# A two-layer RWKV/conv/Fourier/MoE block: the input projection and its sixteen units put in one fixed order on every queue

## Chip, core and metric

One core of a Trainium2 chip runs the whole block in one launch. The metric is the device time of one execution in microseconds (us). Engines: TensorE (PE; PEld is its weight load), VectorE (DVE), ScalarE (ACT), GpSimd (POOL), and SyncE (SP), which here issues nearly all DMA transfers. All data are float32; the projection runs on pairs of fp32r values.

## The reference, cut to what matters

1024 latent and 256 context tokens, D = 1024, two layers. The change lies in the first half of a layer, up to the recurrent scan:

```python
px = hx @ w_in                      # 1024 -> 2944 columns, 23 blocks of 128
zx = zx + (grid_shift(zx) - zx) * mu_shift
r, k, v, lw_f, lw_b, la_f, la_b, lg = split(zx)
kk = k * k_k; kk = kk / max(norm(kk), 1e-12)          # per head of 64
for dn in 2 directions:
    decay = exp(-exp(-softplus(-(w0 + tanh(lw) @ w2)) - 0.5))
    a     = sigmoid(a0 + la @ a2);  k_dir = k * (1 + (a - 1) * k_a)
    S_t = S_{t-1} diag(decay_t) - (S_{t-1} kk_t)(kk_t * a_t)^T + v_t k_dir_t^T;  y_t = S_t r_t
```

Then gated readout, short convolution, Fourier mixing, output projection, and a mixture of experts, none of which the change touches.

## The kernel before

Each layer goes through stages: input projection with units, scan (the rest of the projection, the convolution and the Fourier part run beside it), output projection, experts, combine. The scan is done in chunks of 64 tokens. What a chunk needs is made ahead in **units**: one unit is one pair of heads (p, four of them), one half of the 1280 tokens (hf) and one direction (d), so 16 units per layer and 10 chunks for each of two heads (e) in a unit.

A unit's steps, all inside `inproj`: `gates` (matmuls of the two low-rank inputs, tanh on ScalarE, scaling and a running sum on VectorE, two exponentials), `heads` (normalised kk, once for two units), `factors` (the operands ar and bk of the chunk products; bk's halves are split between VectorE and GpSimd), `attn` (score matmuls, masked into two tiles X; transposes of bk; the DMA writes of ar, X and bk for the scan). The strictly triangular 64x64 block of each chunk must be inverted: `inverse` takes the two 32x32 diagonal blocks of every chunk of three units from a DRAM scratch image (gD), one block per partition, and inverts them by 30 steps of two operations on GpSimd; it writes the blocks back and a transposed copy to a second image (xD). `merge` reads both for one unit and makes the corner of the 64x64 inverse with two rounds of small matmuls. The last four units' blocks are inverted by VectorE (two) and, beside the scan, GpSimd (two).

Between these the projection runs as a stream (`project`, line 386): 23 blocks of 128 columns, each 24 matmuls for 256 tokens and twice 24 for 512, counted as 0.5 and 1. `Pace` hands them out: `free(n)` issues n of them at once, `feed(n)` ties them behind points that the unit's steps have noted (`point`), and `defer` puts small work a given number of matmuls later. Otherwise the order on each engine is settled by a planner's simulated timeline, SyncE's transfers included. `in_order` (used elsewhere) fixes the order of traced instructions on every engine but SyncE.

Per layer the order is: free until the first heads are there and `Q_FIRST` more, then 16 times a unit with `Q_UNIT` matmuls fed behind it (52 and 35 in layer 0, 49 and 24 in layer 1), then the last `attn`, three merges and `Q_TAIL`. In the pool of tiles, X has two buffers (both used by one unit), ar, bk, E, Ei one each; score products, transposes, heads and gates share two PSUM banks (`bank`).

Of the kernel before, what the change touches and what calls it, by code (L numbers as in the profile page):

```python
# [19 lines left out]
P = 128  # L20
# [20 lines left out]
Q_FIRST, Q_UNIT, Q_TAIL, Q_SCAN, Q_LATE, Q_AT = (40, 35), ((52, 35), (49, 24)), ((40, 60, 40), (20, 60, 40)), 10, 40, (1, 8)  # L41
# [7 lines left out]

Q = 32 * C + 32  # L50
U_ = 2 * Q

# [10 lines left out]
class Pace:  # L63
# [8 lines left out]

    HOLD = 1e9
# [17 lines left out]
    def after(self):  # L91
        return self.tc.issue_after(self.last)

    def one(self, ctx):
        cost = self.cost
        try:
            self.cost = self.stream.send(ctx)
        except StopIteration:
            self.cost = None
        for x in self.later:  # L100
            x[0] -= cost
        while self.later and not self.open and (self.cost is None or self.later[0][0] <= 0):
            self.later.pop(0)[1]()
# [20 lines left out]
class K:  # L124
# [30 lines left out]
    def in_order(self):  # L155
# [128 lines left out]
    def weights(self, l, j):  # L284

        hp = self.hp
        wr = hp.tile([P, KD, P], F32, name="wr")
        self.nc.sync.dma_start(wr, self.a["w_in"][l, j])
# [59 lines left out]
    def inproj(self, l, last):  # L348
# [13 lines left out]
        nc.vector.tensor_scalar(om, self.vec("mu", 0, 15), -1.0, 1.0, op0=OP.mult, op1=OP.add)  # L362
        oka = sp.tile([P, 4], F32, name="oka")
        nc.vector.tensor_scalar(oka, self.vec("ka", 0, 4), -1.0, 1.0, op0=OP.mult, op1=OP.add)
# [21 lines left out]
        def project(j, use, ctx=True):  # L386

            wh, wl = self.pre.pop(j) if j in self.pre else self.weights(l, j)
            for c0, n in NCK if ctx else NCK[1:]:
# [11 lines left out]
                pace.open = False  # L401
                between()

# [32 lines left out]
        def shifted(j, name, bufs=1, ctx=True):  # L436
# [14 lines left out]
            else:  # L451
                nc.gpsimd.memset(z[:, :LC], 0.0)
            ts = slice(0, T) if ctx else slice(LC, T)
            nc.scalar.activation(z[:, ts], z[:, ts], AF.Copy, scale=om[:, j:j + 1])
            nc.vector.scalar_tensor_tensor(z[:, ts], zs[:, ts], self.vec("mu", j), z[:, ts], op0=OP.mult, op1=OP.add)
            return z
# [20 lines left out]
        def heads(p, hf, k, inv):  # L477

            kk = un.tile([P, HT], F32, name="kk", bufs=2)
            nc.gpsimd.tensor_copy(kk.rearrange("q (t e d) -> q t e d", e=2, d=64),  # L480
                                 inv[:, 5 * hf:5 * hf + 5, :, None].to_broadcast([P, 5, 2, 64]))
            ps = bank()
            for t in range(5):
                nc.tensor.matmul(ps[:, t * P:(t + 1) * P], kk[:, t * P:(t + 1) * P], self.ident, start=True, stop=True)
# [7 lines left out]
        def gates(p, hf, d, lw, la):  # L492
# [6 lines left out]
            for i, (w, src, dst) in enumerate(((w2, lw, sg), (a2, la, aa))):  # L499
# [8 lines left out]
                nc.vector.tensor_scalar(dst, dst, 0.5, 0.5, op0=OP.mult, op1=OP.add)  # L508
            rev = slice(None, None, -1) if d else slice(None)
            nc.vector.tensor_tensor_scan(flat(sg)[:, rev], rst, flat(sg)[:, rev], 0.0, op0=OP.mult, op1=OP.add)  # L510
            E = un.tile([P, HC, C], F32, name="E")
            Ei = un.tile([P, HC, C], F32, name="Ei")
            nc.scalar.activation(E, sg, AF.Exp, scale=-CC)
            nc.scalar.activation(Ei, sg, AF.Exp, scale=CC)
            return aa, E, Ei

        def factors(p, hf, d, r, k, kk, g, kds):
            aa, E, Ei = g
            rev = slice(None, None, -1) if d else slice(None)
            e0 = 0 if d else C - 1  # L520
            nc.vector.tensor_copy(self.wc[d][:, p, hf * HC:(hf + 1) * HC], E[:, :, e0])
            kd = un.tile([P, HC, C], F32, name="kd", bufs=2)
            nc.scalar.activation(kd, aa, AF.Identity, bias=oka[:, p:p + 1], scale=self.vec("ka", p))
            nc.vector.tensor_tensor(kd, kd, cv(k, hf), op=OP.mult)
            kds.append(kd)
            nc.vector.tensor_tensor(aa, aa, Ei, op=OP.mult)


            ar = un.tile([P, 2, HC, C], F32, name="ar")
            bk = un.tile([P, HC, 2, C], F32, name="bk")  # L530
            lo, hi = slice(0, 64), slice(64, 128)
# [10 lines left out]
            nc.vector.tensor_tensor(ar[:, 1], cv(r, hf), E, op=OP.mult)  # L542
            if len(kds) == 2:
                nc.gpsimd.tensor_tensor(kds[0], kds[0], kds[1], op=OP.add)
                nc.gpsimd.tensor_tensor(kds[0], kds[0], cv(r, hf), op=OP.mult)
# [3 lines left out]
        def attn(p, hf, d, ar, bk):  # L549

            GR = ((0, 5), (5, 5))
            half = lambda e: slice(64 * e, 64 * e + 64)
            img = slice(hf * HC, (hf + 1) * HC)

            Xs = [un.tile([P, 2, HC, C], F32, name="X", bufs=2) for _ in range(2)]
            for c0, n in ((0, 4), (4, 3), (7, 3)):
                ps = bank().rearrange("q (e c s t) -> q e c s t", e=2, s=2, t=C)
                for c in range(n):
                    for e in range(2):
                        h = half(e)  # L560
                        mm = nc.tensor.matmul(ps[:, e, c], bk[h, c0 + c].rearrange("q s t -> q (s t)"), ar[h, :, c0 + c, :],  # L561
                                              start=True, stop=True)
                pace.point(mm, W_ATTN)
                for e in range(2):
                    mv = msk[:, d, e].rearrange("q (s t) -> q s t", s=2)
                    nc.vector.tensor_tensor(Xs[e][:, :, c0:c0 + n].rearrange("q s c t -> q c s t"), ps[:, e, :n],  # L566
                                            mv[:, None].to_broadcast([P, n, 2, C]), op=OP.mult)
            for e in range(2):
                h, o = half(e), half(1 - e)
                X = Xs[e]  # L570
                sn = "q s (n c) t -> q (s n) (c t)"
                for v, rows in ((ar[h], h), (X[o], o)):
                    nc.sync.dma_start(self.rlD[d][e][img, rows, p, :].rearrange("m q x -> q m x"),
                                      v.rearrange(sn, c=2))
                nc.sync.dma_start(self.abD[d][hf * 5:hf * 5 + 5, h, 1, p, :].rearrange("n q x -> q n x"),
                                  X[h, 1].rearrange("q (n c) t -> q n (c t)", c=2))
                m = (2 * place[p, hf, d] + e) * HC
                nc.sync.dma_start(self.mats(self.gD, m, HC), X[h, 0])

            for c0, n in GR:  # L580
                ps = bank()
# [5 lines left out]
                nc.scalar.activation(bt[:, :n].rearrange("q c t -> q (c t)"), ps[:, :n * P], AF.Copy)  # L587
                ch = slice(hf * HC + c0, hf * HC + c0 + n)
                nc.sync.dma_start(self.btD[d][ch, :, p, :].rearrange("c q x -> q c x"), bt[:, :n])

        def inverse(u0, n, eng, new=None):
# [16 lines left out]
            def finish():  # L608
                if new is None:
                    xt = un.tile([P, 32, 32], F32, name="zt")[:n]  # L610
                    nc.scalar.activation(xt, gt.rearrange("q i a -> q a i"), AF.Copy)
                    nc.sync.dma_start(self.diag(self.gD, j0, n), gt)
                else:
                    xs = [qp.tile([P, 512], F32, name=name)[:n].rearrange("q (a i) -> q a i", i=32)
                          for name in ("pq", "pl")]
                    for x, sl in zip(xs, (slice(0, 16), slice(16, 32))):
                        nc.scalar.activation(x, gt[:, :, sl].rearrange("q i a -> q a i"), AF.Copy)
                    nc.sync.dma_start(self.diag(self.gD, j0, n), gt)
                    xt = gt
                    for x, sl in zip(xs, (slice(0, 16), slice(16, 32))):  # L620
                        nc.scalar.activation(xt[:, sl], x, AF.Copy)
                nc.sync.dma_start(self.diag(self.xD, j0, n), xt)
            return finish

        def merge(u, new, bank="pq"):
# [7 lines left out]
            for e, (r, o) in enumerate(ro):  # L633
                m = (2 * u + e) * HC
                nc.sync.dma_start(AM[64 * e:64 * e + 64], self.mats(self.gD, m, HC))
                nc.sync.dma_start(XP[r], self.mats(self.xD, m, HC)[lo, :, lo])

            def work(ctx):
                for st in range(2):
# [10 lines left out]
                    for e, (r, o) in enumerate(ro):  # L650
                        if st == 0:
                            nc.scalar.activation(XP[o], pq[o], AF.Copy)
                        else:
                            nc.scalar.activation(AM[r, :, hi], pq[r], AF.Copy)
                nc.sync.dma_start(self.abD[d][hf * 5:hf * 5 + 5, :, 0, p, :].rearrange("n q x -> q n x"),
                                  AM.rearrange("q (n c) t -> q n (c t)", c=2))
            return work

        def values(p):

            zo = yield from shifted(8 + p, "v")
            nc.sync.dma_start(self.vT[p], zo)

            def late():
# [12 lines left out]
            pace.defer(Q_LATE, late)  # L677
# [90 lines left out]
        def gate():  # L768
            zo = yield from shifted(14, "v", 1, not last)
            nc.scalar.activation(zo, zo, AF.Sigmoid)  # L770
            nc.sync.dma_start(self.lgT, zo)
        cs_, rks, invs = [], [], []

        def streams(p):
            yield from values(p)
            k = yield from shifted(p + 4, "k", 2)
# [1174 lines left out]
```

## Time and profile before

| | us |
|---|---|
| median of 3 runs (3517.28 to 3523.49) | 3521.67 |
| profiled execution | 3517.43 |
| its span (first to last instruction) | 3515.6 |
| mean granted TensorE clock | 0.926 |
| first gates, last masked X, first scan step, layer 0 | 174.5, 583.1, 638.2 |
| the same, layer 1 | 1968.7, 2364.6, 2427.4 |
| busy: PE, DVE, ACT, POOL (share of the span) | 89%, 65%, 53%, 32% |

A busy share is an average over stages with different limits, so the rows below are cut to the stage of the change. The granted clock is given as a share of full speed. DMA share is the mean busy share of the core's 16 DMA engines. SyncE's instructions are not counted as busy; its waits are listed by themselves. A wait is put down to what came last.

### The profile page before, as it was taken

The page shows a single profiled execution, that of the slowest core. Times are in us where ns is not written, and L with a number is a line of the kernel's source. Part 1 is how long each engine was busy: PE and PEld are TensorE (multiplying, and loading weights), DVE is VectorE, ACT ScalarE, POOL GpSimd, SP SyncE. Part 2 cuts the span into 40 slices and gives each one's busy share as a digit, 9 for nine tenths or more (in the row PEclk, how much of TensorE's full clock was granted, in tenths as well). Part 3 has the DMA queues.
Part 4 walks back from the last instruction along what each step waited for, and adds up shares of the span by engine and source line. Part 5 has one row for each costly group of instructions (what it writes and reads, how often), then busy time and mean ns, then how long its engine had stood idle before and what let it go on. Part 6 is the DMA issues. An engine that isn't in the chain of part 4 may idle for free. (4 is left out here: it accounts for less than half of the span.)

```text
span 3515.6 us, 59528 instructions
## 1 busy us (share of the span) xinstructions
PE 3123.8 (89%) x22452; PEld 2447.4 (70%) x22452; DVE 2274.8 (65%) x3543; ACT 1852.3 (53%) x2856; POOL 1140.5 (32%) x1083
## 2 busy tenths in 40 slices
PE   6998889798898999999979988776988989999996
PEld 3776667577676777788746766565776867778883
DVE  4275566233467899988763465554334879998885
ACT  4343433335333777788753434333353457778883
POOL 0026675411222222333200166664013222233330
PEclk8998888899998999999989999877999989999998
DMA  6668889879755999999956678889896478999996
GB/s 248 213 159 174 185 182 195 229 215 329 228 199 188 363 350 337 369 386 381 369 218 213 177 181 189 176 181 236 231 327 198 154 309 317 348 365 378 377 387 232
DMA packets 708060, 922.36 MB, mean 262 GB/s; under 512 B 335074, under 2 KB 561259, under 8 KB 657852
## 3 DMA queue, kind: packets, MB, share of 16 engines
q1 hardware_dynamic: 669456, 871.05, 77.9%
q0 software_dynamic: 38304, 47.49, 4.0%
q8 instruction: 178, 2.92, 0.3%
q14 instruction: 110, 0.90, 0.1%
q10 hardware_dynamic: 12, 0.00, 0.0%
HBM read 726.92 MB, written 203.23 MB: 265 GB/s over the span
## 5 line engine op out<-in xcount | busy, mean ns | idle before, releaser
L176 DVE TENSOR_TENSOR hl<-ld,hl 128x1024 fp32r<-128x1024 f32 x734 | 892.0, 1267 | 39.4 <-ACT hl L175 37.3
L175 ACT ACTIVATE hl<-ld 128x1024 fp32r<-128x1024 f32 x796 | 793.3, 1058 | 23.9 <-PE pR L1571 15.4
L1571 PE MATMUL pR<-hl,wk 128*128 128x512 f32 x1560 | 455.5, 400 | 0.0
L1571 PE MATMUL pU<-hl,wk 128*128 128x512 f32 x1560 | 446.5, 394 | 0.0
L1595 PE MATMUL pA<-hl,wk 128*128 128x512 f32 x1560 | 388.2, 403 | 12.6 <-DVE wk L176 8.2
L397 PE MATMUL pb<-hh,wh 128*128 128x512 f32 (+1 forms) x1000 | 392.0, 393 | 4.1 <-ACT r L430 1.7
L397 PE MATMUL pb<-hh,wl 128*128 128x512 f32 (+1 forms) x1000 | 385.9, 386 | 6.5 <-DVE wl L176 6.5
L397 PE MATMUL pb<-hl,wh 128*128 128x512 f32 (+1 forms) x1000 | 386.4, 387 | 0.0
L1595 PEld LDWEIGHTS pA<-hl,wk 128*128 128x128 f32 x1560 | 290.6, 191 | 97.1 <-ACT wk L175 19.2
L1571 PEld LDWEIGHTS pU<-hl,wk 128*128 128x128 f32 x1560 | 294.2, 189 | 68.1
L1571 PEld LDWEIGHTS pR<-hl,wk 128*128 128x128 f32 x1560 | 288.1, 189 | 61.4 <-ACT wk L175 0.8
L176 POOL TENSOR_TENSOR hl<-ld,hl 128x1024 fp32r<-128x1024 f32 x62 | 174.1, 2809 | 369.8 <-ACT hl L175 369.8
L1602 POOL DMA_INDIRECT yb<-wk,sca x64 | 101.2, 1581 | 462.3 <-ACT wk L1601 446.7
L397 PEld LDWEIGHTS pb<-hh,wh 128*128 128x128 f32 x1000 | 199.9, 200 | 67.6 <-issue 11.5
L1276 PE MATMUL pA<-hl,wk 128*128 128x512 f32 x864 | 223.1, 408 | 7.3 <-ACT wk L175 7.3
L397 PEld LDWEIGHTS pb<-hh,wl 128*128 128x128 f32 x1000 | 200.1, 200 | 42.3 <-DVE wl L176 6.8
L397 PEld LDWEIGHTS pb<-hl,wh 128*128 128x128 f32 x1000 | 200.3, 200 | 37.5 <-issue 9.6
L1276 PEld LDWEIGHTS pA<-hl,wk 128*128 128x128 f32 x864 | 160.4, 192 | 47.9 <-ACT wk L175 7.8
L1100 POOL DMA_DIRECT2D yD<-yt x72 | 57.9, 805 | 405.3 <-ACT yt L1099 367.8
L1088 DVE TENSOR_TENSOR tm<-pR,ST 128x256 f32<-128x256 f32 x76 | 32.0, 422 | 235.0 <-PE pR L1083 216.6
L175 ACT ACTIVATE wk<-pm 128x256 fp32r<-128x256 f32 (+1 forms) x195 | 89.2, 457 | 177.9 <-PE pm L1585 117.4
L561 PE MATMUL ps<-ar,bk 64*128 64x128 f32 x1280 | 124.5, 334 | 55.9 <-DVE X L566 22.8
(426 smaller groups left out, 5423.3 us busy)
## 6 DMA issues: line engine op xcount, KB each, us to landing
ld<-in_exp_gu SPq DMA_DIRECT2D x260, 1024.0 KB
ld<-in_exp_dn SPq DMA_DIRECT2D x130, 1024.0 KB
st<-rlD SPq DMA_DIRECT2D x80, 512.0 KB
wr<-in_w_in SPq DMA_DIRECT2D x46, 512.0 KB
rlD<-ar SPq DMA_DIRECT2D x64, 320.0 KB
rlD<-X SPq DMA_DIRECT2D x64, 320.0 KB
btD<-bt SPq DMA_DIRECT2D x64, 320.0 KB
st<-abD SPq DMA_DIRECT2D x40, 512.0 KB
```

What stands on the lines that cost most here:

```text
L175: nc.scalar.activation(hi, src, AF.Copy)
L176: (eng or nc.vector).tensor_tensor(lo, src, hi.bitcast(F32), op=OP.subtract)
L397: mm = nc.tensor.matmul(ps[:, :n], w[:, k, :], h[:, k, c0:c0 + n], start=(k == 0 and i == 0), stop=(k == KD - 1 and i == 2))
L561: mm = nc.tensor.matmul(ps[:, e, c], bk[h, c0 + c].rearrange("q s t -> q (s t)"), ar[h, :, c0 + c, :], start=True, stop=True)
L1088: nc.vector.tensor_tensor(tm, RS[:, 1], ST[d], op=OP.add)
L1100: nc.gpsimd.dma_start(self.yD[d][:, ch * C:(ch + 1) * C, :], yt.rearrange("q p d -> q (p d)"))
L1276: nc.tensor.matmul(ps, oo[o][:, k, :], w[k][w_][:, fs], start=(k == 0 and q == 0), stop=(k == KD - 1 and q == 2))
L1571: nc.tensor.matmul(o, x.xT[xi][:, kk, :], w[wi][:, k, :], start=(kk == 0 and i == 0), stop=(kk == KD - 1 and i == 2))
L1595: nc.tensor.matmul(x.y[n], x.h[:, hi_, f, :], dw[wi][:, 0, n * 512:(n + 1) * 512], start=(f == 0 and i == 0), stop=(f == 3 and i == 2))
L1602: nc.gpsimd.indirect_dma_start(out=yb, out_offset=bass.IndirectOffsetOnAxis(ap=x.sca, axis=0), in_=o, in_offset=None, bounds_check=2 * T - ...
```

## The change

Everything from the stream's start to the last merge before the scan is traced inside `in_order(True)`, which now covers SyncE's transfers too. The unit is cut into steps with matmuls of the stream between them (`go`, `free`), and each step belongs to a given unit: the gates of unit u+1, the factors and operands of unit u, the attention of unit u-1, the merge of an earlier unit. GpSimd keeps the inversion alone. The scratch image holds whole 32x32 blocks, one after the other; the transposed image and its writes go, and the merge makes the transpose with one more round of matmuls. X's block is written in six pieces (two diagonal blocks and a corner, for each head). Weights are fetched two blocks ahead and split one block ahead. The shifted input is mixed 24 matmuls after its block. Layer-wide numbers: `Q_FIRST` 40, 35 becomes 20, 0, `Q_LATE` 40 becomes 30.

```diff
-    def in_order(self):
+    def in_order(self, issue=False):
...
-            if i.engine == mybir.EngineType.SP:
+            if i.engine == mybir.EngineType.SP and not issue:
                 continue
...
+                if c0 == (0 if ctx else NCK[1][0]):
+                    if at + 1 in raw:
+                        self.pre[seq[at + 1]] = self.parts(raw.pop(at + 1))
+                    if at and at + 2 < len(seq):
+                        raw[at + 2] = self.fetch(l, seq[at + 2])
...
@@ heads
-            nc.gpsimd.tensor_copy(kk.rearrange("q (t e d) -> q t e d", e=2, d=64),
-                                 inv[:, 5 * hf:5 * hf + 5, :, None].to_broadcast([P, 5, 2, 64]))
...
+                for e in range(2):
+                    nc.tensor.matmul(ps[64 * e:64 * e + 64, t * P:(t + 1) * P],
+                                     inv[:, 5 * hf + t, e:e + 1].to_broadcast([P, 64]), self.ident, start=True, stop=True)
...
@@ gates
-                nc.vector.tensor_scalar(dst, dst, 0.5, 0.5, op0=OP.mult, op1=OP.add)
+                if i == 0:
+                    nc.scalar.activation(dst, dst, AF.Copy, bias=0.5, scale=0.5)
+                yield
...
@@ factors, operands
-            nc.gpsimd.tensor_tensor(bk[hi, :, 0, :], kd[hi], Ei[hi], op=OP.mult)
-            nc.gpsimd.tensor_tensor(bk[hi, :, 1, :], kk[hi, :, rev], aa[hi, :, rev], op=OP.mult)
-            nc.vector.tensor_tensor(bk[lo, :, 1, :], kd[lo], Ei[lo], op=OP.mult)
-            nc.vector.tensor_tensor(bk[lo, :, 0, :], kk[lo, :, rev], aa[lo, :, rev], op=OP.mult)
+            nc.vector.scalar_tensor_tensor(bk[:, :, 1], kk[:, :, rev], 0.5, aa[:, :, rev], op0=OP.mult, op1=OP.mult)
+            for e in range(2):
+                h = slice(64 * e, 64 * e + 64)
+                nc.vector.tensor_tensor(bk[h, :, 2 - 2 * e], kd[h], Ei[h], op=OP.mult)
...
-                nc.gpsimd.tensor_tensor(kds[0], kds[0], kds[1], op=OP.add)
-                nc.gpsimd.tensor_tensor(kds[0], kds[0], cv(r, hf), op=OP.mult)
+                nc.vector.tensor_tensor(kds[0], kds[0], kds[1], op=OP.add)
+                nc.vector.tensor_tensor(kds[0], kds[0], cv(r, hf), op=OP.mult)
...
@@ attn
-                m = (2 * place[p, hf, d] + e) * HC
-                nc.sync.dma_start(self.mats(self.gD, m, HC), X[h, 0])
+                m = 2 * place[p, hf, d] + e
+                for b in range(2):
+                    q = slice(32 * b, 32 * b + 32)
+                    nc.sync.dma_start(self.diag(m, b), X[h, 0][q, :, q])
+                nc.sync.dma_start(self.corner(m), X[h, 0][0:32, :, 32:64])
...
-                    mm = nc.tensor.transpose(ps[:, c * P:(c + 1) * P], bk[:, c0 + c].rearrange("q s t -> q (s t)"),
-                                             self.ident)
+                    for e in range(2):
+                        h = half(e)
+                        mm = nc.tensor.matmul(ps[:, e, c], left(e, c0 + c), self.ident[h, h], start=True, stop=True)
...
@@ inverse
-            nc.sync.dma_start(gt, self.diag(self.gD, j0, n))
+            img = self.blocks(j0, n)
+            nc.sync.dma_start(gt, img)
...
-                nc.sync.dma_start(self.diag(self.xD, j0, n), xt)
+                nc.sync.dma_start(img, gt.rearrange("q i a -> q (i a)"))
...
@@ inproj, the loop over units
-        for u, (p, hf, d) in enumerate(units):
...
-            pace.feed(Q_UNIT[last][u > 9])
+        with self.in_order(True):
...
+            for u, (p, hf, d) in enumerate(units):
+                n = Q_UNIT[last][u > 9] / 52
+                a_ = attn(*units[u - 1], *ops) if u else iter(())
+                go(a_, 5)
+                f = factors(p, hf, d, k, g)
+                go(a_, 5, 5)
+                next(a_, None)
+                if u % 3 == 0 and u and u < 15:
+                    if inverting:
+                        inverting()
+                    inverting = inverse(u - 3, 3, nc.gpsimd)
+                elif u == 15:
+                    inverting()
+                pace.free(5 * n)
+                if u % 2 == 0:
+                    kk, kds = heads(p, hf, k, invs[p]), []
+                    pace.free(2 * n)
+                go(a_, 4)
+                ops = operands(p, hf, d, r, kk, f, kds)
+                if merging:
+                    m = merging(nullcontext())
+                    go(m, 6, 6)
+                    self.whole(m)
+                else:
+                    pace.free(12 * n)
+                merging = merge(u - 6, lambda: un.tile([P, 1024], F32, name="zt")) if 6 <= u < 15 else None
+                if u < 15:
+                    g_ = gates(*units[u + 1], *lw)
+                    go(g_, 7, 7)
+                    g = self.whole(g_)
+                else:
+                    pace.free(14 * n)
+            a_ = attn(*units[15], *ops)
+            go(a_, 5, 5, 5, 5, 5)
+            self.whole(a_)
+            inverting = inverse(12, 2, nc.vector, by_l)
+            mg = [merge(9 + i, new, ("pq", "pl")[i % 2]) for i, new in
+                  enumerate((x2, x2, lambda: un.tile([P, 1024], F32, name="bk")))]
+            pace.free(30)
+            for m in mg:
+                m = m(nullcontext())
+                go(m, 6, 6)
+                self.whole(m)
+            pace.free(30)
```

## Rows read from the trace of the kernel before

**Rows 1.** Busy time (instructions) by engine, clock, DMA share, GB/s of four stretches.
```profile
core 0: us, PE busy (x) PEld busy (x) DVE busy (x) ACT busy (x) POOL busy (x), PEclk, DMA share, GB/s
174.00:284.00 110.00, 106.08 (x649) 83.94 (x647) 75.23 (x95) 48.66 (x66) 41.17 (x36) 1.00 0.73 167
284.00:584.00 300.00, 255.74 (x2087) 205.77 (x2088) 177.28 (x226) 118.86 (x170) 218.35 (x264) 0.85 0.85 184
...
1969.00:2069.00 100.00, 98.43 (x602) 76.56 (x602) 70.82 (x94) 44.06 (x60) 34.33 (x30) 1.00 0.70 165
2069.00:2365.00 296.00, 233.67 (x1834) 180.64 (x1833) 172.76 (x217) 107.53 (x155) 211.62 (x247) 0.84 0.83 180
```

**Rows 2.** Three lines, layer 0: ns min/median/max, first and last start, shapes.
```profile
L502 PE MATMUL ps<-lw,w x64: 429/429/533, 174.5 to 542.7; 64*128 64x320 f32 x64
...
L566 DVE TENSOR_TENSOR X<-ps,msk x96: 539/549/692, 195.4 to 583.1; 128x384 f32<-128x384 f32 x64, 128x512 f32<-128x512 f32 x32
...
L1061 PE MATMUL pR<-st,st x640: 222/222/369, 638.2 to 907.9; 128*64 128x64 f32 x160
```

**Rows 3.** The same three lines, layer 1.
```profile
L502 PE MATMUL ps<-lw,w x64: 429/429/899, 1968.7 to 2328.5; 64*128 64x320 f32 x64
...
L566 DVE TENSOR_TENSOR X<-ps,msk x96: 540/549/692, 1990.5 to 2364.6; 128x384 f32<-128x384 f32 x64, 128x512 f32<-128x512 f32 x32
...
L1061 PE MATMUL pR<-st,st x640: 222/222/369, 2427.4 to 2673.2; 128*64 128x64 f32 x160
```

**Rows 4.** Who waited for whom, 174 to 600: us in total, times, longest.
```profile
PEld pq L645 <- DMA zt<-gD: 24.6, 8, 11.7
...
PEld ps L561 <- POOL bk L533: 12.3, 5, 3.7
```

**Rows 5.** TensorE in order of time: start, us, what, count; several stretches.
```profile
227.21 2.29 PE L467 MATMUL pl<-hsel,v 128*128 128x2 f32 x20
...
253.88 1.34 PE L502 MATMUL ps<-lw,w 64*128 64x320 f32 x4
...
403.97 0.82 PE L647 MATMUL pq<-zt 32*32 32x32 f32 x40
...
569.94 0.39 PE L397 MATMUL pb<-hh,wh 128*128 128x512 f32 x1
...
571.08 0.39 PE L397 MATMUL pb<-hh,wl 128*128 128x512 f32 x1
571.39 1.93 PE L561 MATMUL ps<-ar,bk 64*128 64x128 f32 x28
...
577.07 0.94 PE L561 MATMUL ps<-ar,bk 64*128 64x128 f32 x12
577.93 0.77 PE L583 MATMUL ps<-ident,bk 128*128 128x128 f32 x5
```

**Rows 6.** Groups by line, 174 to 600: busy us, mean ns, idle before.
```profile
L605 POOL TENSOR_TENSOR tmp<-gt 120x30 f32<-120x30 f32 (+14 forms) x120 | 81.0, 675 | 8.7
...
L532 POOL TENSOR_TENSOR bk<-kd,Ei 64x640 f32<-64x640 f32 x16 | 31.6, 1976 | 43.9 <-issue 21.5 <-PE ps L583 18.3 <-ACT v L430 3.5
...
L535 DVE TENSOR_TENSOR bk<-kk,aa 64x640 f32<-64x640 f32 x16 | 24.0, 1501 | 0.2
```

**Rows 7.** Issue time of two of SyncE's transfers, 174 to 600 (ns min/median/max).
```profile
L578 SPq DMA_DIRECT2D gD<-X x32: 589/1508/2175, 202.2 to 594.4; - x32
...
L636 SPq DMA_DIRECT2D zt<-xD x18: 522/634/1142, 341.3 to 558.3; - x18
```

**Rows 8.** SyncE's own waits, 174 to 600; the longest and the last.
```profile
SPq L573 <- DVE X L566: 24.6, 11, 5.6
...
SPq L589 <- ACT v L430: 0.2, 1, 0.2
```

More of the change, by code (lines that the diff above doesn't have):

```diff
@@ L71, in __init__ @@
         self.open = False
+        self.pinned = True
     HOLD = 1e9
@@ L101, in one @@
             x[0] -= cost
-        while self.later and not self.open and (self.cost is None or self.later[0][0] <= 0):
+        while self.later and (self.pinned or not self.open) and (self.cost is None or self.later[0][0] <= 0):
             self.later.pop(0)[1]()
@@ L552, in attn @@
             half = lambda e: slice(64 * e, 64 * e + 64)
+            left = lambda e, c: bk[half(e), c, 1 - e:3 - e].rearrange("q s t -> q (s t)")
             img = slice(hf * HC, (hf + 1) * HC)
@@ L633, in merge, with steps @@
             for e, (r, o) in enumerate(ro):
[L634 to L638, printed above, removed]
+                m = 2 * u + e
+                nc.vector.memset(AM[o, :, lo], 0.0)
+                nc.sync.dma_start(AM[r, :, hi], self.corner(m))
+                for b, (rows, cols) in enumerate(((r, lo), (o, hi))):
+                    nc.sync.dma_start(AM[rows, :, cols], self.diag(m, b))
+            def steps(ctx):
+                pq = qp.tile([P, 512], F32, name=bank)[:, :HC * 32].rearrange("q (u t) -> q u t", t=32)
+                for c in range(HC):
+                    for r, o in ro:
+                        with ctx:
+                            nc.tensor.matmul(pq[r, c, :], AM[r, c, lo], self.ident[r, r], start=True, stop=True)
+                        ctx = nullcontext()
+                for r, o in ro:
+                    nc.scalar.activation(XP[r], pq[r], AF.Copy)
+                yield
                 for st in range(2):
@@ L654, in work, with then, late @@
                             nc.scalar.activation(AM[r, :, hi], pq[r], AF.Copy)
+                    if st == 0:
+                        yield
                 nc.sync.dma_start(self.abD[d][hf * 5:hf * 5 + 5, :, 0, p, :].rearrange("n q x -> q n x"),
                                   AM.rearrange("q (n c) t -> q n (c t)", c=2))
-            return work
+            return steps
         def values(p):
-            zo = yield from shifted(8 + p, "v")
-            nc.sync.dma_start(self.vT[p], zo)
-            def late():
+            def then(zo):
+                nc.sync.dma_start(self.vT[p], zo)
+                pace.defer(Q_LATE, lambda: late(zo))
+            def late(zo):
                 for t0 in range(0, NT, 4):
@@ L676, in late @@
                             "(t q) d -> q t d", q=P), vt[:, :n, e, :])
-            pace.defer(Q_LATE, late)
+            yield from shifted(8 + p, "v", then)
         def conv(i):
@@ L832, in inproj @@
                 if u < 15:
-                    inverting = inverse(u - 3, 3, nc.gpsimd)
-                else:
-                    inverting = inverse(12, 2, nc.vector, by_l)
-            if 6 <= u < 15:
-                merging = merge(u - 6, zt)
-            pace.feed(Q_UNIT[last][u > 9])
-        attn(*prev)
-        mg = [merge(9 + i, new, ("pq", "pl")[i % 2]) for i, new in enumerate((x2, x2, lambda: un.tile([P, 1024], F32, name="bk")))]
-        pace.feed(Q_TAIL[last][0])
-        pace.free(Q_TAIL[last][1])
@@ L843, in inproj @@
-        for m in mg:
-            m(pace.after())
-        pace.free(Q_TAIL[last][2])
+                    g_ = gates(*units[u + 1], *lw)
+                    go(g_, 7, 7)
+                    g = self.whole(g_)
+                else:
+                    pace.free(14 * n)
[5 more added lines that the diff above has]
+                  enumerate((x2, x2, lambda: un.tile([P, 1024], F32, name="bk")))]
@@ L861, in beside @@
                 for m in ms:
-                    m(pace.after())
+                    self.whole(m(pace.after()))
             qp.release()
```

170 lines of the change are left out of this document (88 added, 82 removed).

## The prediction

> **What bounds the kernel now.** The change touches one stage of each layer: the input projection with its sixteen units, up to the first scan step. I read it first by stretches, then by the first and last starts of its lines, then by who waited, then piece by piece.
>
> By stretches [rows 1]: for its first 110 us (layer 0) TensorE is busy 106.08 of 110.00 us at a granted clock of 1.00, which is its 2.4 GHz level. In the next 300 us it is busy 255.74 of 300 and the granted clock falls to 0.85 (a mix of the 1.2 and 2.4 GHz levels), while GpSimd rises from 41 of 110 to 218 of 300. Layer 1 repeats it: 98.43 of 100, then 233.67 of 296 at 0.84. What begins between the two stretches is GpSimd's block inversion and, three units behind it, the merges. VectorE is at 177 of 300, the DMA engines at 0.85: neither is full.
>
> By lines: layer 0 has its first gates at 174.5 and its last masked X (L566) at 583.1, so 409 us; the scan (L1061) starts at 638.2, 55 us later [rows 2]. Layer 1: 1968.7, 2364.6 and 2427.4, so 396 and 63 us [rows 3]. That is 25.6 and 24.8 us per unit.
>
> By waits [rows 4]: TensorE's weight loads sat idle 12.3 us for GpSimd's half of bk, and 24.6 us for a merge's tile on its way from the scratch image. These 37 us are most of the 48 us that TensorE is idle from 174 to 584 (3.9 + 44.3) [rows 1]. So the stage is bound by TensorE, plus stalls that GpSimd and scratch traffic cause, plus the slow clock during and after stalls.
>
> **The change, part by part.** I price TensorE's work after the change at the full clock, and then put a stall factor on it.
>
> *Projection.* Five 512-column matmuls follow each other from 569.94 to 571.08 [rows 5], 0.228 us apart. Counting the code's budgets, with the rounding up that its free() makes when the share is a fraction: layer 0 has 343 such matmuls ahead of the first gates (340 before) and 1122 at the end of the last unit's attention; layer 1 has 311 (323 before) and 1020. Between gates and end: 779 x 0.228 = 178 us and 709 x 0.228 = 162 us. When the stage ends the counts are 1212 against 1210 in layer 0, and 1098 against 1077 in layer 1. The scan inherits the same work in layer 0 and 21 matmuls less in layer 1 (some 2 us, as they lie beside the scan's own chain).
>
> *A unit's own matmuls* [rows 5]: scores 28 in 1.93 plus 12 in 0.94 = 2.9 us, unchanged. Gates: 4 in 1.34, eight per unit, unchanged; I take 2.15, as the last one's end overlaps what follows. Transposes of bk: 5 in 0.77, twice, 1.5 us; they become 40 narrower matmuls, at least the same 1.5 and at most the 2.9 of the 40 score matmuls, which are twice as wide; I take 2.5. A merge is 80 small matmuls, 40 in 0.82; one more round makes 120: at least 1.6 if the round hides in gaps, at most 3 x 1.2 with its wait; I take 3.3. Heads go from 10 to 20 matmuls per two units: 0.8 per unit (0.5 to 1.1, by the transposes' price). Norms and value transposes are unchanged: 20 in 2.29 plus some 1.7 us, for three p.
>
> Sum, layer 0: 178 + 16 x (2.9 + 2.15 + 2.5 + 0.8) + 9 x 3.3 + 12 = 353 us. Layer 1: 337. The same sum for the old code is some 311 and 291 us, against 409 and 396 measured: 31 and 36% on top.
>
> *What GpSimd loses.* Both halves of bk there (1976 ns for the first, much the same for the second), the kd pair and the key copy [rows 6]. Its 60 inversion steps per batch, 675 ns mean [rows 6], make 41 us per batch, and a batch has three units: 63 us or more. So no unit waits for it, and the 12.3 us wait goes. What is late next is VectorE.
>
> *What VectorE gains.* One full bk product and, on average, one kd operation per unit, against two scalings that go to ScalarE or into other operations. It now works 177.28/300 x 25.6 = 15.1 us per unit [rows 1]. A product of this length costs 1.50 us [rows 6], so at most 18.1. Below, it may lose 2 us, as GpSimd's 2 us operations no longer run beside it. I take 17, under TensorE's 20 to 24 us, so it costs nothing by itself; it lies behind the matmuls. Without this cover each further us per unit is 32 us.
>
> *What the scratch image changes.* The inversion reads and writes whole 4 KB blocks, and the transposed copy with its write goes. Against it X's block is now written in six pieces rather than two, and a merge reads six rather than four. SyncE's queue issues these in program order. A read of 128 B rows takes 0.63 us to issue, the old write of 256 B rows 1.51 [rows 7]. Six new writes cost 3.8 to 9.1 us against 3.0, and two reads more on 9 of 16 units 0.7. SyncE waited 148 of the 426 us from 174 to 600 (41 rows, first and last of them in [rows 8]), 9.2 us per unit, so at the lower price this is hidden in its waits, and behind it only merges and scan loads queue. I take 4.5 us for the six, as their pieces are half as many bytes as the old ones'.
> The Trainium skill (DMA: Bandwidth & Descriptors, Specifications) speaks against this part: transfers under 512 B pay a read-modify-write, and the new pieces are 128 B. The trace agrees in that the 256 B write is the slowest row of the two; by the rule the six cost the 9.1 us, and the sum is that of the first rival.
>
> *The tail.* The last two inversions before the scan run on VectorE, and now no other work may pass them. They begin some 11 us after the last X (ten X transfers and two of bt on SyncE, then a load) and 60 steps of about 0.37 us make 22 us. In layer 0 the matmul count shows a projection chunk with a VectorE drain behind these steps, while two more chunks and the three merges want its bank: TensorE waits until 34 us, three merges in a row take 21, store and loads 11: the scan starts 66 us after the last X, 55 before: 11 us lost. In layer 1 one merge and a half come ahead of that chunk: 56 us against 63, 7 gained.
>
> *Stalls.* The best stretch now has 3.6% idle, the whole stage 31% over its parts. The two named waits go, and in their place come queues in which each engine waits in program order. I take 10%, nearer to the best stretch as GpSimd is out of the chain. Layer 0: 353 x 1.10 = 388, last X at 175.5 + 388 = 563.5, 20 earlier. Layer 1: 371, from 1966, 28 earlier.
>
> Sum: -20 + 11 - 28 - 7 - 2 = -46 us against the profiled execution's own 3517.4 us (span 3515.6 and 1.8 around it), so 3471. The median of the runs is 4 us above the profiled one: 3475.
>
> **The rivals.**
> *The queue takes it back.* If small writes cost 1.51 each, SyncE gains 6.0 + 0.7 = 6.7 us per unit, while its 9.2 us of waits shrink with the shorter unit by about 2: it has nothing left, and units stay near 25 us. For: the DMA engines stand at 0.85 already, and the merge tiles are waited for now. Against: the inversion's 32-row transfers go. 3500 to 3530.
> *Slower: the fixed order makes the queue's waits add up.* Place: SyncE, behind the ten X transfers; price: 16.4 us of issue per unit (25.6 - 9.2) plus 6.7 plus half of the waits, 4.6, that no other transfer may now fill: 27.7 us, 2.1 more, x 32 = 67, so 3585. It decides from the point at which issue and unfilled waits exceed 25.6 us per unit. VectorE could do the same with 18.1 us plus more than 7.5 us of waits.
> *More gain.* Stalls stay at the 3.6% of the best stretch: 366 and 349 us, -42 and -50, tail as above: 3425. For: that stretch has the same unit without inversion and merges. Against: merges and masks still wait for each other.
> *It doesn't do what it says.* The old order may already be nearly this order, and the slow clock be due to the many small matmuls; then only the tail is left: within 0.2%.
>
> **How the numbers follow.** Forecast (3440 to 3500) 0.50; more gain 0.16; queue or order without effect (3500 to 3530) 0.19; slower 0.15. A measurement of this kernel tells some 0.2%, 7 us, from no change. Faster by more: 0.50 + 0.16 + a little over half of the third, 0.11, is 0.77; same 0.08; slower 0.15. The range 3410 to 3535 leaves out the tails of the second and last case; the likeliest case alone spans 3440 to 3500.
>
> **What would show it.** Right: after the first inversion TensorE's busy share stays over 92% and its clock over 0.95; no wait for GpSimd at the scores; a unit takes 23 to 25 us, 20 to 21 in the last six; GpSimd some 45 us per batch; in layer 0 TensorE idle 10 to 20 us after the last X. Wrong: SyncE without waits and merges late (first rival), VectorE over 90% busy in the units, or a scan that takes longer than its 270 and 246 us.

## The result, and the profile after

The changed kernel takes 3728.57 us (median of 4 runs, 3721.65 to 3739.37) against 3522.58 beside it: 1.0588 times as long [1.0562, 1.0615], 206 us slower, where 47 us faster was forecast.

First its stretches (start:end, length, busy time with instruction counts by engine, granted clock, DMA share, GB/s), which answer to [rows 1]:

```profile
175.00:285.00 110.00, 102.78 (x672) 77.44 (x671) 55.02 (x77) 44.59 (x61) 6.62 (x17) 0.95 0.57 141
285.00:585.00 300.00, 252.53 (x2287) 189.06 (x2289) 144.26 (x200) 107.21 (x163) 131.05 (x207) 0.85 0.61 145
585.00:661.00 76.00, 70.23 (x677) 52.59 (x671) 35.15 (x55) 27.53 (x42) 12.12 (x22) 0.77 0.63 150
661.00:745.00 84.00, 37.58 (x523) 30.32 (x522) 44.78 (x83) 12.97 (x26) 31.99 (x66) 0.70 0.40 90
...
2559.00:2642.00 83.00, 40.46 (x485) 31.09 (x484) 43.27 (x80) 12.27 (x24) 32.07 (x66) 0.61 0.46 109
```

GpSimd, VectorE and the DMA engines are all less busy than in [rows 1], and TensorE is no busier, at the same 0.85: after 300 us the stage is 76 us from its end. Then come 84 us (layer 1: 83) in which TensorE works less than half the time. First gates, masked X and first scan step, against [rows 2] and [rows 3]:

```profile
L524 PE MATMUL ps<-lw,w x64: 429/429/898, 175.0 to 622.0; 64*128 64x320 f32 x64
...
L600 DVE TENSOR_TENSOR X<-ps,msk x96: 542/550/694, 198.8 to 660.6; 128x384 f32<-128x384 f32 x64, 128x512 f32<-128x512 f32 x32
L1145 PE MATMUL pR<-st,st x640: 222/222/369, 745.2 to 1020.2; 128*64 128x64 f32 x160
...
L524 PE MATMUL ps<-lw,w x64: 429/429/898, 2083.7 to 2528.9; 64*128 64x320 f32 x64
...
L600 DVE TENSOR_TENSOR X<-ps,msk x96: 495/549/694, 2110.7 to 2559.1; 128x384 f32<-128x384 f32 x64, 128x512 f32<-128x512 f32 x32
L1145 PE MATMUL pR<-st,st x640: 222/222/369, 2642.1 to 2880.8; 128*64 128x64 f32 x160
```

Gates to last X: 486 us for 409 and 475 for 396. Last X to scan: 85 for 55 and 83 for 63. Together 206 us. The scans (275 and 239 us, for 270 and 246) nearly cancel. VectorE's waits from 175 to 661 us (us in total, times, longest):

```profile
DVE zt L662 <- DMA abD<-zt: 61.1, 7, 11.5
DVE wl L175 <- ACT wh L174: 42.4, 9, 11.6
DVE aa L546 <- ACT kd L545: 25.9, 14, 6.1
```

The first is new. (The second, VectorE's split of a weight block, stood at 9.5 us before; no run takes it by itself.) Line 662 is the merge's memset of a corner of its tile, traced with the merge's loads. The tile zt has one buffer, so the memset waits until the merge before has stored its result from it to abD, a DRAM tensor. What it holds up is seen in VectorE's own order of time (start, us, what, idle before and who ended it):

```profile
435.04 0.76 DVE L662 MEMSET zt<- 32x320 f32 x2 [11.50 <-DMA abD<-zt]
435.82 1.49 DVE L534 TENSOR_TENSOR_SCAN sg<-rst,sg 128x640 f32<-128x640 f32 x1
437.23 1.26 DVE L600 TENSOR_TENSOR X<-ps,msk 128x512 f32<-128x512 f32 x2
439.56 0.82 DVE L546 SCALAR_TENSOR_TENSOR aa<-aa,Ei 128x640 f32<-128x640 f32 x1 [1.06 <-ACT kd L545]
```

The next unit's decay scan (L534) and the masks of scores (L600) follow the memset at once: they stood behind it. In the tail TensorE has one long wait, for VectorE to drain a projection block, that is to copy it out of PSUM (661 to 746 us):

```profile
PE pb L406 <- DVE r L453: 35.5, 1, 35.5
```

### The profile page after: what moved, and what is told of

It is laid out like the page before. It is cut to its first block, busy times and chain, and to the rows that moved or that the text cites. A ratio compares the mean times of both kernels' runs of the same rounds, so it can differ in the third digit from the quotient of the medians.

```text
span 3719.9 us, 64443 instructions
## 1 busy us (share of the span) xinstructions
PE 3278.5 (88%) x24852; PEld 2523.1 (68%) x24852; DVE 2272.5 (61%) x3614; ACT 1878.7 (51%) x2930; POOL 917.2 (25%) x966
## 5 line engine op out<-in xcount | busy, mean ns | idle before, releaser
L406 PE MATMUL pb<-hh,wh 128*128 128x512 f32 (+1 forms) x1000 | 413.7, 414 | 67.8 <-DVE r L453 64.2
L406 PE MATMUL pb<-hh,wl 128*128 128x512 f32 (+1 forms) x1000 | 407.4, 407 | 0.8 <-DVE wl L175 0.8
L406 PE MATMUL pb<-hl,wh 128*128 128x512 f32 (+1 forms) x1000 | 404.7, 405 | 0.0
L406 PEld LDWEIGHTS pb<-hh,wh 128*128 128x128 f32 x1000 | 207.9, 208 | 144.6 <-DVE r L453 64.4
L406 PEld LDWEIGHTS pb<-hh,wl 128*128 128x128 f32 x1000 | 207.6, 208 | 49.3 <-issue 15.9
L406 PEld LDWEIGHTS pb<-hl,wh 128*128 128x128 f32 x1000 | 208.0, 208 | 41.1 <-issue 9.3
L175 DVE TENSOR_TENSOR wl<-wr,wh 128x1024 fp32r<-128x1024 f32 x46 | 57.2, 1243 | 205.0 <-ACT wh L174 204.8
```

What stands on the lines that cost most here:

```text
L175: (eng or nc.vector).tensor_tensor(lo, src, hi.bitcast(F32), op=OP.subtract)
L406: mm = nc.tensor.matmul(ps[:, :n], w[:, k, :], h[:, k, c0:c0 + n], start=(k == 0 and i == 0), stop=(k == KD - 1 and i == 2))
```

## Experiments

Theories at the start: A, VectorE's queue is held by the memset; B, VectorE cannot take GpSimd's work; C, the order on SyncE; D, the tail behind VectorE's inversion. From the runs came B' and N (TensorE's narrow transposes), K (one key buffer), P and V (the fixed order on TensorE, or on ScalarE and VectorE). All ratios are to the kernel before, run beside each.

**Edits to the changed kernel, one after the other.**

`a1_memset`:
```diff
-                nc.vector.memset(AM[o, :, lo], 0.0)      # with the loads
             def steps(ctx):
+                for r, o in ro:
+                    nc.vector.memset(AM[o, :, lo], 0.0)
```


> The changed kernel with one edit: the merge's memset of its tile's lower corner is traced with the merge's first matmuls, a unit later, rather than with the merge's loads. Theory A (VectorE's queue is held by that memset, which waits for the store of the merge before): the 61.1 and 58.1 us that VectorE waited there go, most of them on the path: 3610 to 3650 us, and the spikes of 38 to 47 us per unit fall below 30. Theory B (what GpSimd lost is too much for VectorE): the same busy time is left on VectorE, so no more than 20 us: above 3705. Theory C (the order on SyncE): SyncE still holds the loads of a merge behind the store of the one before, so the wait moves to TensorE: above 3690.

Measured 3643.65 us, 1.0351 [1.0329, 1.0372]: 85 us back, as A said, and none of B's or C's numbers. The wait is gone from the list (its first row is now the one below), and both unit stages are shorter: last X at 624.3 from first gates at 176.2, so 448 us (486 before the edit), and 440 (475).

```profile
DVE wl L175 <- ACT wh L174: 39.1, 8, 10.5
...
L600 DVE TENSOR_TENSOR X<-ps,msk x96: 540/550/694, 200.0 to 624.3; 128x384 f32<-128x384 f32 x64, 128x512 f32<-128x512 f32 x32
```

A's other sign did not come: from gates to gates single units still take up to 36 us in layer 0 and 40 in layer 1. Of the 119 us that the memsets waited in both layers, 73 come back there. The tails stay at 86 and 79 us.

`a3_tail`: the fixed order ends before the last attention.
```diff
-            a_ = attn(*units[15], *ops)     # inside in_order, as all down to the last free
+        pace.pinned = False
+        a_ = attn(*units[15], *ops)
```


> The changed kernel with the fixed order ended after the last unit: the last attention, VectorE's inversion and the three merges are left to the planner, as before. Theory D (the tail lost 29.5 and 20 us because projection drains stand behind the 60 steps of VectorE's inversion): the scan starts 55 to 63 us after the last masked X, and the time falls by 40 to 50 us, to 3680 to 3690. Rival (the tail is late because the merges' loads and stores are): under 15 us gained, above 3713.

3692.73 us, 1.0496 [1.0464, 1.0527]: 36 back, short of 40. The tails are what D forecast, or better:

```profile
L600 DVE TENSOR_TENSOR X<-ps,msk x96: 540/550/694, 199.8 to 662.5; 128x384 f32<-128x384 f32 x64, 128x512 f32<-128x512 f32 x32
L1145 PE MATMUL pR<-st,st x640: 222/222/366, 712.6 to 992.8; 128*64 128x64 f32 x160
...
L600 DVE TENSOR_TENSOR X<-ps,msk x96: 495/548/694, 2083.4 to 2543.0; 128x384 f32<-128x384 f32 x64, 128x512 f32<-128x512 f32 x32
L1145 PE MATMUL pR<-st,st x640: 216/222/369, 2591.6 to 2851.3; 128*64 128x64 f32 x160
```

50 us and 49, for 85 and 83: 69 gained. About half is given back: the scans are 280 and 260 us for 275 and 239, and layer 1's units take 11 us more.

`a4_memset_tail`: both edits.

> The changed kernel with both edits, the memset a unit later and the tail left to the planner. If the two losses are separate they add up: 3729 less 85 less 36, 3608, within 12. If the tail was late because the memsets stood in it too, less: 3620 to 3645.

3612.74 us, 1.0255 [1.0228, 1.0282]: 116 of the 121 that the two give singly. They are separate losses, as forecast (3608, within 12).

`a5_wide`: bk in two columns, so that 10 wide transposes do for 40 narrow matmuls.
```diff
-            bk = un.tile([P, HC, 3, C], F32, name="bk")
-            nc.vector.scalar_tensor_tensor(bk[:, :, 1], kk[:, :, rev], 0.5, aa[:, :, rev], ...)
+            bk = un.tile([P, HC, 2, C], F32, name="bk")
...
+                nc.vector.scalar_tensor_tensor(bk[h, :, e], kk[h, :, rev], 0.5, aa[h, :, rev], ...)
...
-                    for e in range(2):
-                        mm = nc.tensor.matmul(ps[:, e, c], left(e, c0 + c), self.ident[h, h], ...)
+                    mm = nc.tensor.transpose(ps[:, c * P:(c + 1) * P], bk[:, c0 + c]..., self.ident)
```


> The kernel with both edits, and bk in two columns again with 10 wide transposes; VectorE has four half products for a full one and two halves, 0.9 us a unit more. Theory B' (TensorE): 45 less 18, 27 us a layer, go: 3545 to 3560. Theory B (VectorE): 0.9 us a unit more on VectorE, 3605 to 3640.

3590.56 us, 1.0197 [1.0167, 1.0227]: 22 back, less than half of the 54 that B' priced and short of its range, and against B, as VectorE's work grew.

`a6_sp`: the same with `with self.in_order():`, so SyncE is free.

> The kernel with late memset, free tail and wide transposes (3591 us), with the fixed order taken off SyncE's transfers alone. Theory C (the order on SyncE holds transfers behind waits; SyncE waited 48 us for masked X and 32 for a merge's store in layer 0): 3530 to 3560. Rival (the stalls left are those of ScalarE, VectorE and TensorE, each in its own order): 3580 to 3600.

3573.60 us, 1.0134 [1.0111, 1.0158]: 17 back, between the two forecasts. C is a small part.

**Which engine's order.** Three kernels from the last one, the fixed order on fewer engines.
```diff
-        with self.in_order():
+        with self.in_order((SP, DVE, Activation, Pool)):   # a7_pe: these are free
+        with self.in_order((SP, PE)):                      # a8_nope: these are free
+        with nullcontext():                                # a9_free: all are free
```


> The kernel with late memset, free tail, wide transposes and SyncE free (3574 us), with the fixed order on TensorE alone. Theory P (TensorE's fixed order is what is left): no change, 3565 to 3585. Theory V (ScalarE's and VectorE's own order, in which short work stands behind waits for others): most of the 52 to 66 us go, 3510 to 3530.

> The same kernel (3574 us) with the fixed order on VectorE, ScalarE and GpSimd, and none on TensorE and SyncE. Theory P: 3510 to 3535. Theory V: 3565 to 3590.

> The same kernel with no fixed order; the projection's matmuls are not tied to the units' points either, so TensorE takes them in the order of the program where the planner sees them ready. If the order alone is what costs: 3500 to 3530. If the cutting of the unit into steps, the weights fetched ahead and the late mix cost as well: 3550 or more.

TensorE alone ordered: 3584.42, 1.0168 [1.0138, 1.0198]. The others ordered, TensorE not: 3620.16, 1.0265 [1.0229, 1.0302]. None: 3528.91, 1.0013 [0.9994, 1.0032]. The first run fits P's range, though it is some 10 us slower than the kernel that it comes from. The second contradicts P and V alike: a fixed order on the others with TensorE loose beside it is worst of the three, so the parts don't add. But without any order, almost the whole loss is gone, with the unit still cut into steps, the weights fetched ahead and the mix late. It is not gone at every place: from first gates to last X this kernel takes 419 and 440 us, where the kernel before takes 409 and 396, and its way from last X to scan is 40 and 39 us, for 55 and 63. Against the run with SyncE free (447 and 438 us) the stage gains 28 us in layer 0 and nothing in layer 1; the rest comes mostly from the tail of layer 0 (14) and the scan of layer 1 (18).

TensorE ordered (first) and nothing ordered (second), in layer 0 from the first gates to the last X:

```profile
175.00:285.00 110.00, 101.81 (x628) 76.81 (x628) 66.50 (x92) 49.75 (x67) 13.01 (x25) 0.97 0.62 153
285.00:625.00 340.00, 286.02 (x2592) 214.93 (x2591) 189.26 (x267) 131.57 (x202) 155.61 (x221) 0.88 0.67 158
```

```profile
175.00:285.00 110.00, 107.39 (x672) 85.16 (x672) 67.55 (x93) 49.80 (x68) 14.27 (x25) 0.97 0.64 156
285.00:593.00 308.00, 269.68 (x2542) 211.45 (x2541) 188.92 (x260) 129.12 (x198) 159.18 (x221) 0.89 0.74 173
```

Idle: 62 us of 450 against 41 of 418, for nearly the same number of matmuls (3220 and 3214 records). In order, TensorE waited 34 us for masks (23 out of order) and 15 for a merge's drain (none), and nothing behind such an instruction may pass it.

**Parts of the change alone, in the kernel before, under the planner's order.**

`b1_gponly`: bk, key copy and kd pair off GpSimd, as in the change: bk in three columns, narrow matmuls for its transposes, narrow ones for the key copy, one key buffer.

> The kernel before with one part of the change alone: bk, the key copy and the kd pair leave GpSimd (bk with three columns and one shared, transposes as 40 narrow matmuls); the order stays the planner's. Theory B (VectorE cannot take this work): slower than before, 3540 to 3600. Theories A, C and D (the order makes the loss): no slower than before, 3490 to 3525, as the 12.3 us wait at bk goes in each layer and 1 us of matmuls per unit comes in.

3680.21 us, 1.0444 [1.0415, 1.0474]: as slow as B said and slower. But VectorE was not fuller than before, 62 of the first 110 us for 75. So the part was divided:

`b3_narrow`: the layout, the narrow matmuls and one key buffer; GpSimd keeps its products.

> The kernel before with one part of the kernel with GpSimd freed alone: bk in three columns and its transposes as 40 narrow matmuls instead of 10 wide ones; GpSimd keeps its products, the key tile has one buffer as there. Theory B' (TensorE's added work is what costs): the narrow matmuls took 71 ns each in the run with GpSimd freed, 45 us a layer against 18, so 27 us a layer: 3570 to 3590, by the lower clock up to 3640. Theory B (VectorE): the products have not moved, so 3520 to 3530.

`b4_dve`: only the work moved to VectorE, as four half products.
```diff
-            nc.gpsimd.tensor_tensor(bk[hi, :, 0, :], kd[hi], Ei[hi], op=OP.mult)     # and the other four
+            nc.vector.tensor_tensor(bk[hi, :, 0, :], kd[hi], Ei[hi], op=OP.mult)
```


> The kernel before with the other part alone: all of bk, the key copy and the kd pair on VectorE, bk in two columns, wide transposes as before. VectorE gains two half products (0.93 us each) and on average 1.8 us of kd pair and key copy a unit. Theory B (VectorE): most of the 160 us is here, 3600 to 3680. Theory B' (TensorE): the wait for GpSimd's bk, 12.3 us, goes, and nothing comes in on TensorE: 3495 to 3525.

Narrow: 3664.22, 1.0411 [1.0383, 1.0438], above both forecasts. Work moved: 3522.70, 1.0003 [0.9987, 1.0020]. That ends B: VectorE takes it at no cost (and no gain: the last X is 5 us earlier in layer 0, the scan 9 us longer). The 16 us by which b1 is slower than the narrow form alone were not taken apart.

`b5_kk1` (`name="kk", bufs=2` without the `bufs=2`) and `b6_narrow2` (the narrow matmuls alone):

> The kernel before with one buffer for the key tile instead of two, as in the run with narrow transposes, and nothing else. That run lost 144 us where its matmuls explain 54. Theory K (the single key buffer makes GpSimd's copy and products wait for each other, 80.5 us of waits at bk in layer 0): 3580 to 3620. Theory N (the narrow transposes alone, with the stalls and the lower clock that they bring): 3515 to 3530.

> The kernel before with 40 narrow matmuls for the transposes of bk in its two-column layout; the key tile keeps two buffers. Theory N: all of the 144 us, 3650 to 3670. Theory K: the matmuls' own 27 us a layer, 3570 to 3580.

3542.10, 1.0058 [1.0035, 1.0081], and 3663.95, 1.0404 [1.0380, 1.0427]. The second is what N forecast. The first lies between the two forecasts: one key buffer costs 20 us by itself, but nothing on top of the narrow matmuls (3664.22 with it, 3663.95 without). So the loss goes with the narrow matmuls, and it is far more than their own time.

`b7_twice` (the 10 wide transposes done twice) and `b8_half` (the narrow pieces, but by the transpose operation):
```diff
-                        mm = nc.tensor.matmul(ps[:, e, c], bk[h, c0 + c]..., self.ident[h, h], start=True, stop=True)
+                        mm = nc.tensor.transpose(ps[:, e, c], bk[h, c0 + c]..., self.ident[h, h])
```


> The kernel before with each of the 10 wide transposes of bk done twice over into the same place: 160 more matmuls a layer, 18 us by their 0.115 us each, against 27 for the narrow form. If added TensorE time in the chain of the unit brings stalls and a lower clock with it: 3580 or more. If the narrow form is what does it: 18 us a layer, 3550 to 3565.

> The kernel before with each wide transpose of bk done as two, one for each half of the partitions, by the transpose operation, not as a matmul with the identity: 20 a unit against 10. If narrow pieces are what costs (the two halves of the array in turn): 3600 or more. If the matmul form is (40 records a unit, as each float32 matmul shows as two): at most 18 us a layer as in the run with doubled transposes: 3525 to 3560.

3563.09, 1.0110 [1.0078, 1.0141], and 3560.19, 1.0103 [1.0064, 1.0142]. Doing the transposes twice costs its own time and no more: 39 us, and by the spacing of starts the second set takes 19 us a layer. Narrow transposes cost 38 us, though they take no more of TensorE than the wide ones (15 us a layer for 18): so small pieces have a price too, which no run explains. The other 104 of the 142 us come with the matmul form. The records of layer 0's transposes (busy us, mean ns, idle before), wide in the kernel before, then as narrow matmuls and as narrow transposes:

```profile
L583 PE MATMUL ps<-ident,bk 128*128 128x128 f32 x160 | 25.6, 295 | 1.9 <-DVE X L566 1.8
```

```profile
L585 PE MATMUL ps<-ident,bk 64*128 64x64 f32 x620 | 43.0, 288 | 1.3 <-DVE X L566 1.3
```

```profile
L585 PE MATMUL ps<-ident,bk 64*128 64x64 f32 x310 | 16.6, 243 | 4.6 <-DVE lw L610 3.5 <-DVE X L566 1.1
```

The last two: same pieces, same output, twice the records, 2.6 times the busy time. The Trainium skill (Perfetto Trace Analysis, Transposes) says that a transpose should be done as one and not as a standard matmul; these rows agree. By the spacing of starts the matmul form takes 42 us a layer where the wide transposes take 18, yet the layer loses 71. Why 24 become 71 stays open: the waits grow too. From 174 us to the last X, TensorE idles 48 us of 410 in the kernel before [rows 1], and here 84 of 472:

```profile
174.00:284.00 110.00, 99.94 (x660) 80.45 (x660) 66.93 (x84) 44.38 (x60) 30.57 (x26) 0.95 0.63 147
284.00:646.00 362.00, 288.02 (x2528) 236.36 (x2527) 183.71 (x238) 122.62 (x176) 223.40 (x274) 0.82 0.74 161
```

GpSimd's wait before it may write the next bk, until the transposes have read the last, is 65 us here and 18 in the kernel before, but no single waiter explains the loss. Whether the planner chose a worse order for the matmul form was not tried; that the same exchange was worth only 22 us in the fixed order speaks for it.

`b2_image`: the scratch image of the change, its six pieces and the third merge round.

> The kernel before with one part of the change alone: the scratch image holds whole 32x32 blocks, X's block is written in six pieces, the merge reads six and has one more round of matmuls (its memset traced with its matmuls); the order stays the planner's. If small pieces are what costs: 6.7 us of SyncE per unit are not hidden, 3560 to 3700. If they are hidden, as the prediction took: 25 merges with one more round, about 1.2 us each, are 30 us at most, less what the simpler read of the inversion gives back: 3500 to 3550.

3524.68 us, 1.0018 [1.0004, 1.0032]: the small pieces are hidden.

**A version that beats both.** `c1_dve_image` joins b4 and b2; `c2_first` also takes the change's 20 and 0 matmuls ahead of the gates.

> The kernel before with the two parts that cost nothing alone: GpSimd only inverts (wide transposes), whole blocks in the scratch image; the order stays the planner's. If the parts are separate: 3518 to 3530, no different from before. If each hides a limit of the other (GpSimd's wait in the image run, 19.9 us; the wait for scratch in the other): 3490 to 3510, below both kernels.

> The kernel of two parts under the planner's order (3508 us) with one number of the change besides: 20 and 0 matmuls ahead of the first gates for 40 and 35. The stage starts 4.6 and 8 us earlier and hands these matmuls to later stretches. If these have room in stalls: 3495 to 3503. If TensorE is full there and the scan gets them: 3505 to 3515.

c1: 3507.83 us, 0.9966 [0.9947, 0.9985], 14 us under the kernel before beside it and 221 under the changed one. That is 0.3%, small but clear of its interval, and inside the forecast for two parts that hide each other's limit; why they gain together what neither does alone was not taken apart. c2: 3513.84, 0.9983 [0.9964, 1.0002], no gain, as forecast where TensorE is full. In c1 the first stretch of each layer is at clock 1.00, as in the kernel before, and TensorE is idle 40 of 401 us in layer 0:

```profile
175.00:285.00 110.00, 106.61 (x648) 83.44 (x648) 78.87 (x111) 47.97 (x64) 16.68 (x23) 1.00 0.67 163
285.00:576.00 291.00, 254.36 (x2462) 204.65 (x2462) 192.38 (x276) 120.16 (x186) 163.74 (x222) 0.89 0.77 178
```

## Why the prediction was wrong

Down the ladder the 206 us are: memset and tail 116, narrow transposes 22, SyncE's order 17, the order on the other engines 45; what is left, some 5 us, can't be told from none. The steps hold for this sequence of edits, as the parts don't add up in every one (the three runs on which engine's order). 178 of the 206 came back where an edit freed an engine from waiting in the fixed order, a part that the prediction priced with 10% of its sum and, for the tail, with 11 us less 7.

- **The failed step is the stall factor.** The prediction says "in their place come queues in which each engine waits in program order. I take 10%": the figure leans on the best stretch of the old order, and no row prices the new waits. The two waits that it named did go from TensorE's list, but against its own sum of 353 us layer 0's stage took 486: 38% on top, more than the 31% of the old code. What took their place is VectorE's 61 us at the memset, in the queue behind which masks and scans stood, and TensorE's own waits in order. With memset, tail, transposes and SyncE mended it still took 447, and 419 without an order.
- **VectorE "costs nothing by itself"**: right for its work (b4; in the changed kernel some 15 us busy a unit, not 17), wrong for its queue. The merge's memset, an operation that the change adds (the cut diff leaves it out), is not in the prediction at all, nor is the single buffer that it waits for.
- **The terms of the sum** nearly held. By the spacing of starts in layer 0, a unit's transposes take 2.9 us (2.5 taken), gates 2.8 (2.15), scores 3.1 (2.9), heads 0.7 (0.8), a merge 2.7 (3.3), norms and values 10 in all (12): 188 us for 175. The projection took 232 us for 178, and 68 us lie in gaps over 0.9 us (52 in the kernel before, counted alike): 13 + 54 + 68 is the difference from 353 to 486, within 2. A part of the 54 is the clock: it was granted at the lower level (1.2 GHz) for 133 of the 486 us, in 14 pieces, 11 of them right behind a wait of TensorE; 512-column matmuls start 0.43 us apart in them and 0.23 outside (medians). So the sum of TensorE's work at the full clock was nearly right, with its 42 us of new work, and what it was multiplied with was not.
- **The tail** had the right mechanism, too small: 85 and 83 us for 66 and 56, TensorE's wait 35.5 for 10 to 20. Layer 1 has no advantage.
- **GpSimd**: right. No wait for it at the scores, batches of 41 to 45 us, as forecast.
- **The scratch image**: right (b2). SyncE issues a 128 B row piece in 0.52 us:

```profile
L609 SPq DMA_DIRECT2D gD<-X x62: 302/522/1767, 211.2 to 661.1; - x62
```

That is a third of the 1.51 of [rows 7], so the rival "the queue takes it back" fell. The prediction took the rule of the Trainium skill (DMA: Bandwidth & Descriptors, Specifications), that transfers under 512 B pay a read-modify-write, for the upper price, and saw the trace agree. But the old 256 B rows lie under 512 B as well, so that row could not bear the rule out, and the issue time of the smaller pieces does not show it.
- **The rival "slower"** had the mechanism and the sign, at 0.15, but the wrong engine. Its place was SyncE, worth 17 us; VectorE (memset, tail) and the order on the other engines carried the rest. Its half sentence on VectorE was nearest: it asked for 7.5 us of waits a unit, and VectorE is idle some 16 (234 us busy in the 486), though 10 of these it had before.
- **A slip**: by its own terms (-42 + 11 - 50 - 7 - 2) the rival "more gain" comes to 3431, not 3425. Nothing rests on it.
- **What would show it**: units of 30.4 us (486 / 16), not 23 to 25; busy 84% and clock 0.85 after the first inversion, not 92% and 0.95.

## What to carry to other kernels

Before an order is fixed on a queue, list for each instruction that waits on a transfer or a reused buffer what stands behind it: here two memsets of 0.76 us together, once a merge, cost 85 us, and all the work moved to VectorE nothing. A fixed order on TensorE alone left the mended kernel at 3584 us, none at all at 3529: it takes away the fill of the gaps, so ready matmuls must be placed where the waits are, or the order left loose. Try the parts of a change one by one: two of these together gained, and one operation's form (a transpose written as a matmul) hid in the third.

## What the runs showed of the hardware

- One 64x640 product on VectorE (L535) took 1.50 us in the kernel before [rows 6]. With GpSimd's products moved it takes 0.93 us (b4) and 0.94 (c1): there 0.87 in the first 110 us of the stage and 0.98 in the rest, where GpSimd is busy 164 of 291 us, almost all of it inversion. The row of c1 (busy us, mean ns):

```profile
L535 DVE TENSOR_TENSOR bk<-kk,aa 64x640 f32<-64x640 f32 x16 | 15.1, 944 | 0.1
```

The Trainium skill (SBUF — State Buffer, Terms) tells of a port pair that VectorE and GpSimd hold by turns, and the rows agree, though no run here tests the port apart. The shorter products fit with how little the five moved operations cost VectorE: it is busy 17.0 us a unit in c1 (271 us to the last X) for 15.8 before (253, [rows 1]).
- A transpose of a 64-row piece of float32 leaves one record, and the next starts 47 ns later (b8). The same piece as a matmul with the identity leaves two, 66 ns apart (b6).
